# Layer 1's scores in a two-layer decoder trunk: the second half of the queries against all keys as three float32r products, on one core of a Trainium2 chip

## The chip, the cores and the metric

The kernel runs on one core of one Trainium2 chip. The metric is the device time of one execution in microseconds (us), as a median over runs. A core has five engines with a queue each, worked off in order: TensorE (PE: matrix products, into PSUM only), VectorE (DVE), ScalarE (ACT), GpSimd (POOL) and SyncE (SP, which here issues the loads). They run side by side and wait for each other by semaphores.

## The reference

A trunk of two layers over 256 tokens of 2048 features, all in float32. Each layer is a token mixer and a gated channel mixer. Layer 0's mixer is block attention, which for 256 tokens is plain causal attention; layer 1's is multi-head latent attention, and the change is there:

```python
cq = rms_norm(h @ wq_a, g_qa)
q = (cq @ wq_b).reshape(B, S, H, NOPE + RD)
q_nope = rms_norm(q[..., :NOPE], g_qn)
q_rope = rope(rms_norm(q[..., NOPE:], g_qr), pos, RD)
...
kv = (ckv @ wkv_b).reshape(B, S, H, NOPE + VD)
k_nope = rms_norm(kv[..., :NOPE], g_kn)
v = kv[..., NOPE:]
s = (jnp.einsum('bqhd,bkhd->bhqk', qn, k_nope)
     + jnp.einsum('bqhr,bkr->bhqk', qr, k_rope)).astype(F32) * scale
s = jnp.where(pos[None, :] <= q_pos[:, None], s, NEG_INF)
p = jax.nn.softmax(s, axis=-1).astype(v.dtype)
```

There are 16 heads with 128 plain and 64 rotary features each, and 128 value features.

## The kernel before

**Products and quanta.** Weights stream in from memory. A piece of 128 x 512 weights is split into a float32r part (`whi`, cast by ScalarE, L104) and the rest (`wlo`, subtracted by VectorE, L105); activations are split the same way. A product of full precision is then three float32r products: high by high, high by rest, rest by high. The work is a list of 1464 quanta, one piece each. Before quantum q, `ws.split` issues the casts of pieces up to four ahead; then come the quantum's matmuls (six of 512 columns in `tok_major`, L239, or twelve of 256 columns in `feat_major`, L265 to L267); then whatever was planned for this quantum: `first_in(q, ...)` (softmax transposes, values) ahead of `at(q, ...)`, and these in the order in which they were planned. Each engine's instructions stand in the order in which this loop issues them.

**Layer 1's attention** goes in four groups of four heads. A group has three or four kinds of four quanta each: keys, queries, values (the first group: queries, a half of the rotary queries, keys, values). Let K be the last quantum of a group's keys; its queries end at K+4, its values at K+8 and the next group's keys at K+12. For keys and for queries, `plan_heads` (L640) plans:

- `evac` (L365) at the kind's last quantum: ScalarE copies the two accumulators into a tile `qk`. There are two such tiles (L368, `bufs=2`), taken in turn by keys and queries.
- `squares` (L380) in the two quanta after it: four VectorE instructions for each half of the tokens, each with a readout, square and sum the heads one by one. (The first queries have a longer plan, `wide`.)
- `rstd` (L401) three quanta after it, on VectorE and GpSimd, and `scaled` (L411), on VectorE, five and six quanta after.
- `turned` (L455) and `turned_out` (L467) nine quanta after for heads 0 and 1, ten after for heads 2 and 3: four transposes into one PSUM bank `tp`, which one ScalarE instruction copies out with the gain, 128 x 512, into the tile `room`. There are two `tp` banks (`ps_tp`, `bufs=2`), and all transposes use them.

`room` takes the place of the tile `h`, which held the normed input; in it lie two sets of queries and keys, for even and odd groups, and three sets of values.

**A head** (`Head.plan`, L571): `scores` (L487) at quantum Q = K+15, +18, +21, +24 for the four heads of a group. For layer 1 the loop at L497 takes queries 0 to 127 by keys 0 to 127 and queries 128 to 255 by all 256 keys; each is one float32 product (L499), which PE runs in two passes, and two float32r products of the rotary part (L504). Then: masked maximum (`biased`, VectorE) at Q, `exps` (ScalarE) at Q+1, `normal` (VectorE) at Q+2, the transposes of the probabilities (`turn`, L533, into a `tp` bank; `turned`, L539, ScalarE copies them out) at Q+6, and `values` (L552) with `parted` at Q+9.

Layer 0 has its scores in three products already: `scores` has a branch for it (`self.parts`, L491 to L496), and `queries_out` (L603) and `keys_out` (L612) copy a bank out in three steps: ScalarE the high part, ScalarE a plain copy for the first half, VectorE the rest, `tp` minus the high part.

Of the kernel before, what the change touches and what calls it, by code (L numbers as in the profile page):

```python
# [48 lines left out]
BY_TOKEN, BY_FEATURE = (8, 8), (24, 56)  # L49

H_START = 8


class Stream:
# [61 lines left out]
def trunk(ctx: ExitStack, tc: tile.TileContext, a, out):  # L116
# [100 lines left out]
    def at(q, f, *args):  # L217
        side.setdefault(q, []).append((f, args))
# [51 lines left out]
    class Norm:  # L270
# [86 lines left out]
    class Heads:  # L357


        def __init__(self, state, n_heads, dh, gain, rot, tabs, scale, gain_column=None):  # L360
            self.gain_column = gain_column
# [26 lines left out]
        def squared(self):  # L388

            self.sq = []  # L390
            for t in range(NT):
                sq = att_pool.tile([P, 16 * 32], F32, name="ro2", bufs=2)
                nc.scalar.activation(sq, self.x[:, t].rearrange("p n d -> p (n d)"), AF.Square)
                self.sq.append(sq.rearrange("p (n d) -> p n d", n=self.n))

# [13 lines left out]
            nc.gpsimd.tensor_tensor(self.r, ms, mhalf[:, : NT * n], op=ALU.pow)  # L409

        def scaled(self, t):  # L411
            if self.gain_column is not None or self.gain is None:
                r = self.r[:, t * self.n : (t + 1) * self.n]
                nc.vector.tensor_tensor(
                    self.x[:, t], self.x[:, t], r[:, :, None].to_broadcast([P, self.n, self.dh]),
                    op=ALU.mult,
                )
                return
            g = gains[:, self.gain : self.gain + self.dh]
            for i in range(self.n):  # L420
                c = t * self.n + i
                nc.vector.scalar_tensor_tensor(
                    self.x[:, t, i], self.x[:, t, i], self.r[:, c : c + 1], g,
                    op0=ALU.mult, op1=ALU.mult,
                )
# [38 lines left out]
                    )  # L464
            pair["tp"] = tp

        def turned_out(self, dst, pair, i0):  # L467
            o = dst[:, i0 : i0 + 2, :].rearrange("p a s -> p (a s)")
            if self.gain_column is None:
                nc.scalar.copy(o, pair["tp"])  # L470
            else:
                c = self.gain_column
                nc.scalar.activation(o, pair["tp"], AF.Copy, scale=par[:, c : c + 1])

    def three(o, w_hi, w_lo, m_hi, m_lo, start, stop):

        mm(o, w_hi, m_hi, start=start, stop=False)  # L477
        mm(o, w_hi, m_lo, start=False, stop=False)  # L478
        mm(o, w_lo, m_hi, start=False, stop=stop)  # L479


    class Head:
# [4 lines left out]
        def scores(self):  # L487
            sc = ps_sc.tile([P, 512], F32, name="sc")
            qT, kT, i = self.qT(), self.kT(), self.i
            self.sc = sc  # L490
            if self.parts:  # L491

                (q0, q1), (k0, k) = qT, kT
                mm(sc[:, :P], q0[:, i], k0[:, i], start=True, stop=True)  # L494
                three(sc[:, P : 3 * P], q1[:, 0, i], q1[:, 1, i], k[:, 0, i], k[:, 1, i], True, True)
                return  # L496
            for q0, n, c in ((0, P, 0), (P, S, P)):  # L497
                o = sc[:, c : c + n]
                mm(o, qT[:, i, q0 : q0 + P], kT[:, i, :n], start=True, stop=self.rope is None)  # L499
                if self.rope is not None:  # L500

                    qr, kr = self.rope()
                    for part in range(2):
                        mm(o, qr[:, q0 : q0 + P], kr[:, part, :n], start=False, stop=part == 1)  # L504

        def biased(self):
            self.s = att_pool.tile([P, 3 * P], F32, name="s", bufs=3)
# [104 lines left out]
    def keys_out(dst, tp, i0):  # L612
# [4 lines left out]
        nc.scalar.copy(hi, src)  # L617
        nc.scalar.copy(k0[:, i0 : i0 + 2], src[:, :, :P])
        nc.vector.tensor_tensor(lo, src, hi.bitcast(F32), op=ALU.subtract)

    def evac_parts(state, key, scale):
        v0, v1 = env[key]
# [14 lines left out]
            else:  # L637
                nc.scalar.activation(dst, src, AF.Copy, scale=scale()[:, t : t + 1])

    def plan_heads(q, hs, key, step, out=None, late=0, wide=False):  # L640

        at(q, hs.evac)
        if wide:
            for t in range(NT):
                for i in (0, 2):
                    at(q + 1 + 2 * t + i // 2, hs.squares, t, range(i, i + 2))
                at(q + 8 + t, hs.scaled, t)
            at(q + 5, hs.rstd)
            for i0 in (0, 2):
                pair = {}  # L650
                q1 = q + 11 + i0 // 2
                at(q1, lambda p=pair, i0=i0: hs.turned(env[key], p, i0))
                at(q1, lambda p=pair, i0=i0: hs.turned_out(env[key], p, i0))
            return
        for t in range(NT):
            at(q + step * (1 + t), hs.squares, t)
        at(q + step * 3, hs.rstd)
        for t in range(NT):
            at(q + step * (5 + t) + late * (1 + t), hs.scaled, t)
            at(q + step * (5 + t) + late * (2 + t), hs.rotate, t)  # L660
        for i0 in (0, 2):
            pair = {}
            q1 = q + step * 9 + i0 // 2 + 2 * late
            at(q1, lambda hs=hs, p=pair, i0=i0, key=key: hs.turned(env[key], p, i0))
            if out is None:
                at(q1, lambda hs=hs, p=pair, i0=i0, key=key: hs.turned_out(env[key], p, i0))
            else:
                at(q1, lambda p=pair, i0=i0, key=key: out(env[key], p["tp"], i0))

    at(-1, n1.scaled, 0)  # L670
    at(9, load_constants)
    for g in range(4):
        for kind in "qkv":
# [13 lines left out]
            if kind == "v":  # L687
                at(q, evac_parts, state, ("v", g), lambda: n1.rstd)
                q_v = q
            else:  # L690
                hs = Heads(state, 4, P, G_Q if kind == "q" else G_K, 32, (tab, T_MC, T_MS), lambda: n1.rstd)
                plan_heads(q + (0 if g else 15 if kind == "q" else 9), hs, ("qT" if kind == "q" else "kT", g), 1,
                           queries_out if kind == "q" else keys_out, 1)
                q_k = q
        for i in range(4):
            hd = Head(
# [378 lines left out]
    at(q + 13, kr_turn)  # L1075

    def mla_tiles(g):
        i = 4 * (g % 2)
        env["qT", g] = env["room"][:, i : 4 + i]
        env["kT", g] = env["room"][:, 8 + i : 12 + i]  # L1080
        i = 4 * (g % 3)
        env["v", g] = env["room"][:, 16 + i : 20 + i].rearrange("p (t c) s -> p t (c s)", t=NT)

    for g in range(4):
        for kind in "kqv" if g else "qrkv":
            if kind == "r":
                rotary_queries(1, (6, 10, 12, 15, 16, 17, 18, 20, 21, 23, 24, 25, 26, 28, 40))
                continue
            state = {}
            for kt in range(4):  # L1090
                q = add(tok_major, state, lambda kind=kind: env["cqT" if kind == "q" else "ckvT"], kt, 3)
            if kind == ("k" if g else "q"):
                at(q, mla_tiles, g)
            if kind == "v":
                at(q, evac_values, state, ("v", g), None)
            else:
                q_q = q
                hs = Heads(state, 4, P, None, 0, None, (lambda: cq["scale"]) if kind == "q" else None,
                           C_GQN if kind == "q" else C_GKN)
# [143 lines left out]
```

## Time and profile before

| | us |
|---|---|
| median of 3 runs (2088.34 to 2089.35) | 2088.68 |
| the profiled execution | 2088.1 |
| its span, first to last instruction | 2086.1 |
| PE busy | 2081.1 |
| VectorE busy | 1407.1 |
| ScalarE busy | 1133.3 |

A line of a group reads: line of the kernel, engine, operation, output <- inputs, shapes, count | busy time in us, mean ns of one | idle time of the engine before it, and what ended that. In the chain of waits a line is: start, length, engine, tile, line of the kernel, count; lengths there run from end to end. In a timeline a length is the instruction's own, and instructions that follow each other overlap a little.

### The profile page before, as it was taken

How to read it: one execution, taken by the hardware profiler on the slowest of the kernel's cores; microseconds unless marked ns; L12 is line 12 of the kernel's file. 1: busy time of each engine (PE TensorE's matmuls, PEld its weight loads, DVE VectorE, ACT ScalarE, POOL GpSimd, SP SyncE). 2: the span in 40 equal slices, each digit the busy share in tenths (PEclk: the TensorE clock that was granted, in tenths of full speed). 3: DMA queues.
4: the chain of work that ended last, by engine and by line, in shares of the span. 5: the costliest groups of instructions: out<-in, count | busy, mean ns of one | idle time of the engine just before them, and what ended most of it. 6: DMA issues, size and time to landing. Idle time of an engine off the chain costs nothing.

```text
span 2086.1 us, 42075 instructions
## 1 busy us (share of the span) xinstructions
PE 2081.1 (100%) x16716; PEld 2012.4 (96%) x16716; DVE 1407.1 (67%) x3012; ACT 1133.3 (54%) x2199; POOL 46.1 (2%) x35
## 2 busy tenths in 40 slices
PE   9999999999999999999999999999999999999999
PEld 7888889999999999999999889999999999999999
DVE  6777776776666766655556886776676666755554
ACT  6555555555555555555455666655555555544443
POOL 0000000000000000000000110000000000000000
PEclk9999999999999999999999999999999999999999
DMA  7454445555555555555554533555555555555553
GB/s 274 162 182 176 168 162 202 183 194 190 202 186 200 191 194 199 191 197 189 197 202 154 200 122 122 183 201 185 200 193 191 200 187 200 190 202 208 195 207 132
DMA packets 59381, 391.81 MB, mean 188 GB/s; under 512 B 6960, under 2 KB 10032, under 8 KB 13232
## 3 DMA queue, kind: packets, MB, share of 16 engines
q1 hardware_dynamic: 59040, 388.87, 52.6%
q8 instruction: 130, 2.13, 0.4%
q14 instruction: 67, 0.55, 0.1%
q10 hardware_dynamic: 144, 0.26, 0.0%
HBM read 387.01 MB, written 2.10 MB: 187 GB/s over the span
## 4 chain that ended last, share of the span: by engine, by line
PE 99%; DMA 0%; SPq 0%; DVE 0%; ACT 0%; issue 0%
PE acc L265 26%; PE acc L267 26%; PE acc L266 26%; PE acc L239 17%; PE tp L462 1%; PE sc L499 1%; PE tp L536 1%; PE sc L561 0%; PE sc L504 0%; DMA xT<-in_xT 0%; PE sc L478 0%; PE sc L479 0%; PE sc L477 0%; PE sc L559 0%; PE sc L494 0%; PE sc L562 0%
## 5 line engine op out<-in xcount | busy, mean ns | idle before, releaser
L105 DVE TENSOR_TENSOR wlo<-raw,whi 128x512 fp32r<-128x512 f32 (+1 forms) x1464 | 999.5, 690 | 390.2 <-ACT whi L104 387.6
L104 ACT CAST whi<-raw 128x512 fp32r<-128x512 f32 (+1 forms) x1463 | 869.1, 619 | 456.3 <-PE acc L266 212.5
L265 PE MATMUL acc<-h,whi 128*128 128x256 f32 x2880 | 796.1, 276 | 0.0
L267 PE MATMUL acc<-h,wlo 128*128 128x256 f32 x2880 | 795.7, 276 | 0.0
L266 PE MATMUL acc<-h,whi 128*128 128x256 f32 x2880 | 795.6, 276 | 0.0
L266 PEld LDWEIGHTS acc<-h,whi 128*128 128x128 f32 x2880 | 540.8, 188 | 0.0
L267 PEld LDWEIGHTS acc<-h,wlo 128*128 128x128 f32 x2880 | 540.8, 188 | 0.0
L265 PEld LDWEIGHTS acc<-h,whi 128*128 128x128 f32 x2880 | 540.8, 188 | 0.0
L265 PE MATMUL acc<-a,whi 128*128 128x256 f32 x1408 | 389.0, 276 | 0.0
L266 PE MATMUL acc<-a,whi 128*128 128x256 f32 x1408 | 389.0, 276 | 0.0
L267 PE MATMUL acc<-a,wlo 128*128 128x256 f32 x1408 | 388.9, 276 | 0.0
L239 PE MATMUL acc<-whi,h 128*128 128x512 f32 (+1 forms) x896 | 272.6, 380 | 0.0
L267 PEld LDWEIGHTS acc<-a,wlo 128*128 128x128 f32 x1408 | 264.4, 188 | 0.0
L265 PEld LDWEIGHTS acc<-a,whi 128*128 128x128 f32 x1408 | 264.4, 188 | 0.0
L266 PEld LDWEIGHTS acc<-a,whi 128*128 128x128 f32 x1408 | 264.4, 188 | 0.0
L239 PEld LDWEIGHTS acc<-whi,h 128*128 128x128 f32 x896 | 164.8, 188 | 30.2 <-ACT whi L104 0.7
L239 PE MATMUL acc<-wlo,h 128*128 128x512 f32 (+1 forms) x448 | 168.8, 377 | 0.5 <-DVE wlo L105 0.5
L265 PE MATMUL acc<-oT,whi 128*128 128x256 f32 x512 | 142.7, 279 | 0.0
L267 PE MATMUL acc<-oT,wlo 128*128 128x256 f32 x512 | 141.7, 277 | 0.0
L266 PE MATMUL acc<-oT,whi 128*128 128x256 f32 x512 | 141.7, 277 | 0.0
L770 DVE TENSOR_TENSOR g<-acc,rstd_b 128x256 f32<-128x256 f32 x88 | 37.5, 426 | 125.4 <-PE acc L267 122.4
L777 ACT ACTIVATE c<-g,par 128x256 f32<-128x256 f32 x88 | 53.1, 603 | 108.3 <-DVE g L770 108.3
(163 smaller groups left out, 1599.6 us busy)
## 6 DMA issues: line engine op xcount, KB each, us to landing
raw<-in_ffn_gu SPq DMA_DIRECT2D x176, 1024.0 KB, 4.8
raw<-in_ffn_down SPq DMA_DIRECT2D x88, 1024.0 KB, 4.8
raw<-in_moba_wk SPq DMA_DIRECT2D x16, 1024.0 KB, 4.8
raw<-in_moba_wv SPq DMA_DIRECT2D x16, 1024.0 KB, 4.8
raw<-in_moba_wo SPq DMA_DIRECT2D x16, 1024.0 KB, 4.8
raw<-in_mla_wo SPq DMA_DIRECT2D x16, 1024.0 KB, 4.8
raw<-in_moba_wq SPq DMA_DIRECT2D x13, 1024.0 KB, 4.8
raw<-in_mla_wkv_a SPq DMA_DIRECT2D x8, 576.0 KB, 3.8
```

Source lines behind the costliest of these rows:

```text
L104: self.nc.scalar.copy(hi[:, :n], w)
L105: self.nc.vector.tensor_tensor(lo[:, :n], w, hi[:, :n].bitcast(F32), op=ALU.subtract)
L239: mm(state["acc"][t][:, :n], src[:, kt, c : c + P], (t_lo if part == 1 else t_hi)[:, :n], start=kt == 0 and part == 0, stop=kt == k_last a ...
L265: mm(o, w_hi, src[:, kt, :S], start=first and k == 0, stop=False, skip_group_check=True)
L266: mm(o, w_hi, src[:, kt, S:], start=False, stop=False, skip_group_check=True)
L267: mm(o, w_lo, src[:, kt, :S], start=False, stop=kt == k_last, skip_group_check=True)
L462: nc.tensor.transpose(tp[:, (i * NT + t) * P : (i * NT + t + 1) * P], flat[:, t, c : c + P], ident)
L499: mm(o, qT[:, i, q0 : q0 + P], kT[:, i, :n], start=True, stop=self.rope is None)
L536: nc.tensor.transpose(tp[:, c * P : (c + 1) * P], self.s[:, c * P : (c + 1) * P], ident)
L770: nc.vector.tensor_tensor(self.g[:, 2:], self.gate["acc"][:, :S], self.norm.rstd_b, op=ALU.mult)
L777: nc.scalar.activation(self.c, self.g[:, 2:], AF.Identity, bias=par[:, cb : cb + 1], scale=self.cw(2))
```

## The change

The plain scores of layer 1 take the form that layer 0 has: queries 0 to 127 by keys 0 to 127 stay one float32 product, queries 128 to 255 by all keys become three float32r products. So queries and keys are copied out in parts, with their gain (`queries_out`, `keys_out`). The squares are taken by ScalarE, a whole half of the tokens at once, and summed by one VectorE instruction. The tile `h` is split in two; its first half becomes `room` (plain queries, keys, values) and its second `rparts` (the parts), each with one place for queries and one for keys. A new plan, `plan_latent`, says when the steps run; the transposes of the second rotary queries run one quantum later.

```diff
+class Halves:
+    def __getitem__(self, at):
+        p, k, s = at
+        return self.tiles[k // 8][p, k % 8, s]
...
-                t = keep.tile([P, KD * 2 * S + 64], F32R, name="h")
-                self.h = t[:, H_START : H_START + KD * 2 * S].rearrange("p (k s) -> p k s", k=KD)
+                n = KD // 2 * 2 * S
+                tiles = [keep.tile([P, n + 64], F32R, name=f"h{i}") for i in range(2)]
+                self.h = Halves([
+                    t[:, H_START : H_START + n].rearrange("p (k s) -> p k s", k=KD // 2) for t in tiles
+                ])
...
-                sq = att_pool.tile([P, 16 * 32], F32, name="ro2", bufs=2)
+                sq = att_pool.tile([P, 16 * 32], F32, name="sq" if self.dh == P else "ro2", bufs=2)
                 nc.scalar.activation(sq, self.x[:, t].rearrange("p n d -> p (n d)"), AF.Square)
...
-            for q0, n, c in ((0, P, 0), (P, S, P)):
-                o = sc[:, c : c + n]
-                mm(o, qT[:, i, q0 : q0 + P], kT[:, i, :n], start=True, stop=self.rope is None)
-                if self.rope is not None:
-
-                    qr, kr = self.rope()
-                    for part in range(2):
-                        mm(o, qr[:, q0 : q0 + P], kr[:, part, :n], start=False, stop=part == 1)
+            (q0, q1), (k0, k) = qT, kT
+            first_, second = sc[:, :P], sc[:, P : 3 * P]
+            last = self.rope is None
+            flags = {} if last else {"skip_group_check": True}
+            mm(first_, q0[:, i], k0[:, i], start=True, stop=last, **flags)
+            three(second, q1[:, 0, i], q1[:, 1, i], k[:, 0, i], k[:, 1, i], last, last, **flags)
+            if last:
                 return
+            qr, kr = self.rope()
+            for o, t, n in ((first_, 0, P), (second, 1, S)):
+                for part in range(2):
+                    mm(
+                        o, qr[:, t * P : (t + 1) * P], kr[:, part, :n],
+                        start=False, stop=part == 1, **flags,
+                    )
...
+    def rest_of(lo, src, hi, gain):
+        if gain is None:
+            nc.vector.tensor_tensor(lo, src, hi.bitcast(F32), op=ALU.subtract)
+        else:
+            nc.vector.scalar_tensor_tensor(
+                lo, src, gain, hi.bitcast(F32), op0=ALU.mult, op1=ALU.subtract
+            )
...
-    def queries_out(dst, tp, i0):
+    def queries_out(dst, tp, i0, gain=None):
         q0, q1 = dst
         src = tp.rearrange("p (a t s) -> p a t s", a=2, t=NT)
         hi, lo = q1[:, 0, i0 : i0 + 2], q1[:, 1, i0 : i0 + 2]
-        nc.scalar.copy(hi, src[:, :, 1])
-        nc.scalar.copy(q0[:, i0 : i0 + 2], src[:, :, 0])
-        nc.vector.tensor_tensor(lo, src[:, :, 1], hi.bitcast(F32), op=ALU.subtract)
+        copied(hi, src[:, :, 1], gain)
+        copied(q0[:, i0 : i0 + 2], src[:, :, 0], gain)
+        rest_of(lo, src[:, :, 1], hi, gain)
...
     def open_room():
-        t = keep.tile([P, KD * 2 * S + 64], F32, name="room", tag="h")
-        env["room"] = t[:, : 32 * S].rearrange("p (k s) -> p k s", k=32)
+        n = KD // 2 * 2 * S
+        t = keep.tile([P, n + 64], F32, name="room", tag="h0")
+        env["room"] = t[:, :n].rearrange("p (k s) -> p k s", k=n // 512)
+        t = keep.tile([P, n + 64], F32R, name="rparts", tag="h1")
+        env["rparts"] = t[:, H_START : H_START + 3072].rearrange("p (k s) -> p k s", k=6)
...
+    def plan_latent(q, hs, key, out, sums, rest, turns):
+        at(q, hs.evac)
+        at(q + 1, hs.squared)
+        for t in range(NT):
+            at(q + sums + t, hs.sums, t)
+            at(q + rest + (2 if rest < 5 else 3) + t, hs.scaled, t)
+        at(q + rest, hs.rstd)
+        for i0, turn in zip((0, 2), turns):
+            pair = {}
+            at(q + turn, lambda p=pair, i0=i0: hs.turned(None, p, i0))
+            at(q + turn, lambda p=pair, i0=i0: out(env[key], p["tp"], i0))
...
-                rotary_queries(1, (6, 10, 12, 15, 16, 17, 18, 20, 21, 23, 24, 25, 26, 28, 40))
+                rotary_queries(1, (6, 10, 12, 15, 16, 17, 18, 20, 21, 23, 24, 25, 26, 29, 41))
...
-                plan_heads(q, hs, ("qT" if kind == "q" else "kT", g), 1, wide=(g, kind) == (0, "q"))
+                c, put, turns = (
+                    (C_GQN, queries_out, (9, 12)) if kind == "q" else (C_GKN, keys_out, (10, 14))
+                )
+                if g == 0:
+                    turns = (11, 12) if kind == "q" else (9, 10)
+                plan_latent(
+                    q, hs, ("qT" if kind == "q" else "kT", g), with_gain(put, c), 2,
+                    5 if (g, kind) == (0, "q") else 3, turns,
+                )
```

`keys_out` changes as `queries_out` does, with a high part and a rest of 128 x 512. The remaining lines drop arguments that nothing uses any more.

More of the change, by code (lines that the diff above doesn't have):

```diff
@@ L51, with __init__ @@
 H_START = 8
+class Halves:
+    def __init__(self, tiles):
+        self.tiles = tiles
+    def __getitem__(self, at):
+        p, k, s = at
+        return self.tiles[k // 8][p, k % 8, s]
 class Stream:
@@ L357, in trunk, with __init__ @@
     class Heads:
-        def __init__(self, state, n_heads, dh, gain, rot, tabs, scale, gain_column=None):
-            self.gain_column = gain_column
+        def __init__(self, state, n_heads, dh, gain, rot, tabs, scale):
             self.state, self.n, self.dh, self.gain = state, n_heads, dh, gain
@@ L411, in scaled @@
         def scaled(self, t):
-            if self.gain_column is not None or self.gain is None:
+            if self.gain is None:
                 r = self.r[:, t * self.n : (t + 1) * self.n]
@@ L465, in turned, with three @@
             pair["tp"] = tp
[L467 to L479, printed above, removed]
+    def three(o, w_hi, w_lo, m_hi, m_lo, start, stop, **flags):
+        mm(o, w_hi, m_hi, start=start, stop=False, **flags)
+        mm(o, w_hi, m_lo, start=False, stop=False, **flags)
+        mm(o, w_lo, m_hi, start=False, stop=stop, **flags)
     class Head:
@@ L601, in moba_tiles, with copied @@
         )
-    def queries_out(dst, tp, i0):
+    def copied(dst, src, gain):
+        if gain is None:
+            nc.scalar.copy(dst, src)
+        else:
+            nc.scalar.activation(dst, src, AF.Copy, scale=gain)
+    def rest_of(lo, src, hi, gain):
+        if gain is None:
+            nc.vector.tensor_tensor(lo, src, hi.bitcast(F32), op=ALU.subtract)
+        else:
+            nc.vector.scalar_tensor_tensor(
+                lo, src, gain, hi.bitcast(F32), op0=ALU.mult, op1=ALU.subtract
+            )
+    def queries_out(dst, tp, i0, gain=None):
         q0, q1 = dst
@@ L616, in keys_out @@
         hi, lo = k[:, 0, i0 : i0 + 2], k[:, 1, i0 : i0 + 2]
-        nc.scalar.copy(hi, src)
-        nc.scalar.copy(k0[:, i0 : i0 + 2], src[:, :, :P])
-        nc.vector.tensor_tensor(lo, src, hi.bitcast(F32), op=ALU.subtract)
+        copied(hi, src, gain)
+        copied(k0[:, i0 : i0 + 2], src[:, :, :P], gain)
+        rest_of(lo, src, hi, gain)
     def evac_parts(state, key, scale):
@@ L638, in evac_values, with plan_heads @@
                 nc.scalar.activation(dst, src, AF.Copy, scale=scale()[:, t : t + 1])
-    def plan_heads(q, hs, key, step, out=None, late=0, wide=False):
+    def plan_heads(q, hs, key, out):
         at(q, hs.evac)
[L643 to L654, printed above, removed]
         for t in range(NT):
-            at(q + step * (1 + t), hs.squares, t)
-        at(q + step * 3, hs.rstd)
+            at(q + 1 + t, hs.squares, t)
+        at(q + 3, hs.rstd)
         for t in range(NT):
-            at(q + step * (5 + t) + late * (1 + t), hs.scaled, t)
-            at(q + step * (5 + t) + late * (2 + t), hs.rotate, t)
+            at(q + 6 + 2 * t, hs.scaled, t)
+            at(q + 7 + 2 * t, hs.rotate, t)
         for i0 in (0, 2):
             pair = {}
[L663 to L668, printed above, removed]
+            q1 = q + 11 + i0 // 2
+            at(q1, lambda hs=hs, p=pair, i0=i0: hs.turned(None, p, i0))
+            at(q1, lambda p=pair, i0=i0, key=key: out(env[key], p["tp"], i0))
     at(-1, n1.scaled, 0)
@@ L691, in trunk @@
                 hs = Heads(state, 4, P, G_Q if kind == "q" else G_K, 32, (tab, T_MC, T_MS), lambda: n1.rstd)
-                plan_heads(q + (0 if g else 15 if kind == "q" else 9), hs, ("qT" if kind == "q" else "kT", g), 1,
-                           queries_out if kind == "q" else keys_out, 1)
+                plan_heads(q + (0 if g else 15 if kind == "q" else 9), hs, ("qT" if kind == "q" else "kT", g),
+                           queries_out if kind == "q" else keys_out)
                 q_k = q
@@ L1077, in mla_tiles, with with_gain @@
     def mla_tiles(g):
[L1078 to L1082, printed above, removed]
+        room, parts = env["room"], env["rparts"]
+        env["qT", g] = (
+            room[:, 0].rearrange("p (i s) -> p i s", i=4),
+            parts[:, 4:6].rearrange("p k (i s) -> p k i s", i=4),
+        )
+        env["kT", g] = (
+            room[:, 1].rearrange("p (i s) -> p i s", i=4),
+            parts[:, :4].rearrange("p (k a) (b s) -> p k (a b) s", k=2, b=2),
+        )
+        i = 2 * (1 + g % 3)
+        env["v", g] = room[:, i : i + 2]
+    def with_gain(out, c):
+        return lambda dst, tp, i0: out(dst, tp, i0, par[:, c : c + 1])
+    def plan_latent(q, hs, key, out, sums, rest, turns):
[9 more added lines that the diff above has]
+            at(q + turn, lambda p=pair, i0=i0: out(env[key], p["tp"], i0))
     for g in range(4):
```

11 lines of the change are left out of this document (4 added, 7 removed).

## The prediction

> **What bounds the kernel now.** I read the page first: how busy each engine is, and the chain that ended last.
>
> ```profile
> span 2086.1 us, 42075 instructions
> ...
> PE 2081.1 (100%) x16716; PEld 2012.4 (96%) x16716; DVE 1407.1 (67%) x3012; ACT 1133.3 (54%) x2199; POOL 46.1 (2%) x35
> ...
> PE 99%; DMA 0%; SPq 0%; DVE 0%; ACT 0%; issue 0%
> ```
>
> PE is the bound from end to end. A change gains only what it takes off PE's own instructions, and loses whatever makes PE wait. So I went to the stage that is changed and asked how much room the others have there: busy time in a window, and who waits for whom.
>
> ```profile
> 1174.00:1283.00 109.00, 108.99 (x648) 95.63 (x648) 90.48 (x340) 77.47 (x179) 18.97 (x9) 1.00 0.37 131
> ...
> ACT s L519 <- DVE sst L515: 18.7, 13, 4.1
> ...
> PEld tp L462 <- DVE qk L414: 0.2, 1, 0.2
> ```
>
> The first row has PE, weight loads, VectorE, ScalarE, GpSimd: of 109 us VectorE works 90.5 and ScalarE 77.5. PE waits for next to nothing (0.2 us once, from 1180 to 1300, where no row names a load either), but VectorE is 83% full, and ScalarE's idle time is mostly waiting (18.7 us for softmax sums alone). A shifted order can make PE wait here.
>
> **The change part by part. What PE gains.** The chain, at a head of layer 0 and at one of layer 1:
>
> ```profile
> 83.74 0.12 PE sc L477
> 83.85 0.12 PE sc L478
> 83.97 0.12 PE sc L479
> ...
> 1240.58 0.43 PE sc L561 x2
> 1241.01 0.22 PE sc L562 x2
> 1241.23 0.33 PE tp L536 x3
> 1241.56 0.22 PE sc L499 x2
> 1241.78 0.18 PE sc L504 x2
> 1241.96 0.48 PE sc L499 x2
> 1242.44 0.23 PE sc L504 x2
> ...
> 1244.49 1.38 PE acc L239 x6
> 1245.87 0.44 PE tp L462 x4
> ```
>
> The second L499 (256 columns, float32, two passes) becomes three products at 0.12, 0.36 us. It takes 0.48 in the chain, but the same form of product takes 0.43 at L561, where its neighbours are of its own kind, and L504 ahead of it (0.18 where its second pair has 0.23) looks too short by as much. So each of 16 heads gains between 0.07 and 0.12 us; I take 0.08, nearer to L561: 1.3 us in all, ends 1.1 and 1.9. Transposes keep their number.
>
> **What ScalarE and VectorE get.** From the groups by form, and PE's transpose, for later:
>
> ```profile
> L473 ACT ACTIVATE room<-tp,par 128x512 f32<-128x512 f32 x16 | 11.0, 686 | 5.1 <-PE tp L462 5.1
> L928 ACT ACTIVATE ckvT<-tp,par 128x256 fp32r<-128x256 f32 x4 | 1.9, 475 | 2.3 <-PE tp L923 2.3
> L393 ACT ACTIVATE ro<-qr 128x512 f32<-128x512 f32 x2 | 1.2, 638 | 0.0
> ...
> L383 DVE CUSTOM_DVE_ANT_0 junk<-qk 128x128 f32<-128x128 f32 x64 | 14.9, 286 | 0.0
> L929 DVE SCALAR_TENSOR_TENSOR ckvT<-tp,par,ckvT 128x256 fp32r<-128x256 f32 x4 | 1.9, 485 | 0.5 <-ACT ckvT L928 0.2
> L397 DVE TENSOR_REDUCE ss<-ro 128x8 f32<-128x512 f32 x3 | 2.0, 678 | 0.0
> ...
> L462 PE MATMUL tp<-ident,qk 128*128 128x128 f32 x128 | 19.2, 273 | 0.0
> ```
>
> And a stretch of ScalarE's timeline, with one row of VectorE's:
>
> ```profile
> 1236.01 0.37 ACT L568 CAST oT<-sc 128x256 fp32r<-128x256 f32 x1
> 1236.27 0.49 ACT L542 COPY pT<-tp 128x384 f32<-128x384 f32 x1
> ...
> 1238.20 0.40 ACT L519 ACTIVATE s<-s,sst 128x128 f32<-128x128 f32 x1 [0.34 <-DVE sst L515]
> ...
> 1239.09 0.67 ACT L473 ACTIVATE room<-tp,par 128x512 f32<-128x512 f32 x1
> 1239.66 1.13 ACT L104 CAST whi<-raw 128x512 fp32r<-128x512 f32 x2
> ...
> 1241.97 1.08 ACT L376 COPY qk<-acc 128x512 f32<-128x512 f32 x2
> 1242.92 0.64 ACT L104 CAST whi<-raw 128x512 fp32r<-128x512 f32 x1
> ...
> 1240.30 0.69 DVE L105 TENSOR_TENSOR wlo<-raw,whi 128x512 fp32r<-128x512 f32 x1 [0.34 <-ACT whi L104]
> ```
>
> Queued back to back, an instruction occupies ScalarE 0.10 us less than its length (0.67, but the next starts 0.57 later). VectorE starts 0.03 after the first cast (0.62 long) ends: I take 0.03 for each hand-over.
>
> ScalarE: 16 squares at 0.54 (L393) add 8.6; 16 copies at 0.58 go, -9.3; for queries 16 copies of 128 x 256 at 0.37 (L928) add 6.0; for keys eight of 512 at 0.59 and eight of 256 at 0.37 add 7.7: 13.0 us more, 77.5 to 90.5 of some 108. VectorE: 64 squares at 0.21 (row 1203.71 below to 1204.56, four in 0.85) go, -13.6; 16 sums at 0.68, eight rests of 256 at 0.49 and eight of 512 at 0.73 (between 0.49 and twice that) add at most 20.6: 7.0 more at most. Both still fit on average; what counts is the order.
>
> **The wait that the new plan makes.** In the groups after the first, keys are turned 10 and 14 quanta after K, their last quantum; until now it was 9 and 10. The next group's keys are evacuated at K+12, into the `qk` tile of these keys, since two tiles are used in turn by keys and queries. So ScalarE's evacuation at K+12 must wait for PE's transposes of heads 2 and 3 at K+14; the changed program's instruction order, read engine by engine, has that wait. The evacuation of this place is row 1241.97; K+14's transposes end at 1245.87 + 0.44. ScalarE stands for about 4.3 us, in the third and the fourth group's evacuations: twice.
>
> What is queued behind it: the next cast, the exponentials of K+13, and the copies of queries 0 and 1, turned at K+13 into a `tp` bank. In the old form that bank was free after one copy; now it is free only after ScalarE's high part, ScalarE's plain copy and VectorE's rest. PE needs it for a head's softmax transposes at K+15 (the other bank holds keys 2 and 3). From the end of K+14's transposes: 0.03 + two evacuations 0.95 (1241.97 to 1242.92) + cast 0.51 + exponentials 0.89 (1238.20 to 1239.09) + high part 0.37 + plain copy 0.48 + 0.03 + rest 0.49 + 0.03 = 3.78 us until PE may start, and its first transpose ends 0.27 later, at 4.05. Without the wait PE would do six products of K+15 (1.38) and the values (0.43 + 0.22), and the first transpose would end 0.11 on, at 2.14. PE stalls **1.91 us, twice: 3.8**. Ends: 1.4 with exponentials half done before the stop (VectorE delivers their sums early), 2.4 where another cast slips between.
>
> What is late next: queries 2 and 3, turned at K+16, need the bank that the softmax transposes filled, free when ScalarE has copied the probabilities. ScalarE, from 3.13 (its plain copy, overlap off): two squares 1.08, cast 0.51, keys' high part 0.59, plain copy 0.37, cast 0.51, L568 0.26, L542 0.49, hand-over 0.03: 6.97, first transpose done at 7.24. PE: 4.05 + two transposes 0.22 + scores 1.03 + six products 1.38 + 0.11 = 6.79. Another **0.45, twice: 0.9** (ends 0 and 1.4). Further lateness of the same kind I put at 0.3 (0 to 0.6).
>
> **Casts that come late.** In the first group nothing is reused too early, but the squares stand between casts. The tightest place there, in four timeline rows:
>
> ```profile
> 1206.37 0.40 ACT L519 ACTIVATE s<-s,sst 128x128 f32<-128x128 f32 x1 [4.13 <-DVE sst L515]
> ...
> 1203.71 0.28 DVE L383 CUSTOM_DVE_ANT_0 junk<-qk 128x128 f32<-128x128 f32 x1
> ...
> 1204.56 0.68 DVE L105 TENSOR_TENSOR wlo<-raw,whi 128x512 fp32r<-128x512 f32 x1
> ...
> 1205.67 0.39 PE L239 MATMUL acc<-wlo,ckvT 128*128 128x512 f32 x1
> ```
>
> `wlo` is ready at 1205.24, PE takes it at 1205.67: 0.43 spare. New ahead of it: two squares on ScalarE (1.08); on VectorE the keys' rest and two sums (about 2.0) in place of eight squares (1.70). 1.4 later, less the spare 0.43: I take 0.9 (0, if idle time takes the squares in, to 1.6).
>
> The rest costs nothing: splitting `h` moves addresses by 64 elements with the same loads and matmuls, SP's weight loads keep their order, and GpSimd's powers and the rotary steps their number; the rotary transposes only run a quantum later, with PE's full queue as their cover, and if a bank is late there they are part of the 0.3.
>
> **The sum.** Stalls 3.8 + 0.9 + 0.3 + 0.9 = 5.9, less 1.3: +4.6 us on the profiled execution, 2088.1 (span 2086.1, 2.0 around it) to 2092.7. The median of the runs is 0.6 above that execution, so I forecast 2093.3.
>
> **The rivals.** *Absorbed:* ScalarE's stop costs PE nothing, because casts are up to four pieces ahead. For it: row 1206.37, where ScalarE idles 4.13 us and PE does not wait. Against it: there no bank hung on ScalarE. It decides if the bank for K+15 is free within 2.0 us of K+14's transposes: then PE keeps its gain, 2088.7 - 1.3 = 2087.4, not slower.
>
> *ScalarE becomes the bound:* its idle time is 31.5 us; the two stops take 8.6, and if the 18.7 of waiting for sums stays, 4.2 are left for 13.0 of new work. 8.8 lost, less 1.3: 2096.2. For it: VectorE, which gives those sums, gets no emptier. Against it: waits shrink when the waiting engine comes later.
>
> *The clock drops in the stalls.* At the very start PE ran slower, and at the end it stood still:
>
> ```profile
> 1.19 4.41 PE L176 MATMUL sc<-zeros 128*128 128x512 bf16 x10 [1.19 <-DVE zeros L173]
> ...
> 2084.00:2086.00 2.00, 0.00 (x0) 0.00 (x0) 0.00 (x0) 0.00 (x0) 0.00 (x0) 1.00 0.19 66
> ```
>
> Ten products of 512 columns took 4.41, where ten at 0.23 (six in 1.38) take 2.3: 2.1 us for a cold start. After each long stall that would be 4.2 in all, 2097.4. Against it: the granted clock is 1.00 in every window, also with PE idle for 2 us at the end. The Trainium skill (TensorE: Matmul & The Clock Gate, Part 1: The HAM clock gate) states that the clock halves only after an idle window of about 3.4 us; by that rule stalls of 1.9 us leave it up and this rival falls, and the trace agrees as far as its 1.00 goes.
>
> *The products don't get cheaper* (gain 0, where the shorter form pays for its first product's weights): 2093.3 + 1.3 = 2094.6. Against it: 0.12 each at layer 0.
>
> **How the numbers follow.** Forecast 0.62, own range 2091.3 to 2095.3; absorbed 0.18; ScalarE the bound 0.14; clock 0.03; no cheaper products 0.03. The range of 8 in 10 is 2089.0 to 2097.0: part-absorbed stalls below, the second rival above. About 0.2% (4.2 us) is what a measurement can tell from no change: slower begins at 2092.9, inside the forecast's range. Slower: 0.38 of the forecast, and the three rivals above it, 0.20, 0.58. Same: the forecast's 0.24 and 0.16, 0.40. Faster 0.02.
>
> **What would show it.** PE waiting about 1.9 us twice, some 29 us apart, at transposes of `s`, released by VectorE's new rest; ScalarE idle over 4 us ahead of a `qk` copy, ended by PE's `tp`; three score products at 0.12. No PE waits in layer 1's attention, or waits on `whi` and `wlo` alone, would prove it wrong.

## The result, and the profile after

The changed kernel takes 2094.45 us in the median of 9 runs (2093.31 to 2095.01), the kernel before 2088.68 (9 runs, 2088.34 to 2090.05): a ratio of 1.0026 (95% interval 1.0017 to 1.0035), slower by 5.8 us. The profiled execution took 2094.45 as well, with a span of 2092.4, 6.3 more than before.

From the page after: the span, the busy time of each engine, and the shares of the chain that ended last.

```profile
span 2092.4 us, 42044 instructions
...
PE 2081.6 (99%) x16732; PEld 2011.6 (96%) x16732; DVE 1411.8 (67%) x2916; ACT 1144.9 (55%) x2231; POOL 46.0 (2%) x35
...
PE 98%; ACT 1%; DVE 1%; DMA 0%; SPq 0%; issue 0%
```

PE is still the bound. It is as busy as before (2081.6 against 2081.1), while the span grew by 6.3: PE lost its time by standing still, and the chain now runs over ScalarE and VectorE for 2% of the span.

To see where, take two places that both kernels pass once: the first transposes of `ckv` ahead of layer 1's attention, and the last head's values behind it. The chain of waits of before (start, length, engine, tile, line), with the first and last score row of one late head between them:

```profile
1168.49 0.22 PE tp L923 x2
...
1294.57 0.22 PE sc L499 x2
...
1295.45 0.24 PE sc L504 x2
...
1307.35 0.43 PE sc L561 x2
```

The same of after:

```profile
1169.51 0.22 PE tp L932 x2
...
1294.89 0.22 PE sc L502 x2
1295.11 0.12 PE sc L482
...
1295.35 0.12 PE sc L484
1295.47 0.46 PE sc L510 x4
...
1313.70 0.43 PE sc L570 x2
```

Between the two places lie 138.86 us before and 144.19 after: **+5.33, and all of the change is in there**. I call this time the *stretch* from here on. The 1.02 by which the first place itself is later arose in the first 24 us, while the first loads came in; that it is scatter between runs is shown by a run below. One head's scores take 1.04 us (1294.89 to 1295.93) where they took 1.12: 0.08 gained, and the second and third product start 0.12 apart.

Who waits for whom after, from 1170 to 1310 (us in total, times, longest):

```profile
ACT qk L389 <- PE tp L475: 5.4, 2, 3.0
PEld tp L545 <- DVE rparts L623: 4.2, 3, 2.0
PE tp L545 <- DVE rparts L623: 3.5, 2, 1.8
...
PEld acc L250 <- DVE wlo L116: 2.1, 5, 0.9
...
PEld tp L475 <- ACT pT L551: 0.6, 1, 0.6
...
PE acc L250 <- DVE wlo L116: 0.5, 1, 0.5
```

These are the rows that the prediction named: ScalarE's evacuation into `qk` waits for PE's transposes, twice; PE's softmax transposes wait for VectorE's new rest, twice 1.8 us; and PE waits once for a late `wlo`. PE's timeline at the three places (in brackets the idle time, which counts only from the modelled end of the row above it):

```profile
1206.08 0.61 PE L250 MATMUL acc<-whi,ckvT 128*128 128x512 f32 x2
1207.18 0.50 PE L250 MATMUL acc<-wlo,ckvT 128*128 128x512 f32 x1 [0.48 <-DVE wlo L116]
...
1222.00 0.38 PE L571 MATMUL sc<-pT,room 128*128 128x128 f32 x2
1224.15 0.55 PE L545 MATMUL tp<-ident,s 128*128 128x128 f32 x3 [1.76 <-DVE rparts L623]
...
1251.88 0.38 PE L571 MATMUL sc<-pT,room 128*128 128x128 f32 x2
1254.03 0.55 PE L545 MATMUL tp<-ident,s 128*128 128x128 f32 x3 [1.77 <-DVE rparts L623]
```

From start to start L571 takes 2.15 where it takes 0.22 undisturbed: two stalls of 1.93 us, 29.9 us apart. The late `wlo` costs 1.10 less two products of 0.23: 0.64. So much of the stretch adds up: 3.86 + 0.64 - 1.28 (16 heads at 0.08) = 3.22 of 5.33. The other 2.11 were not added up one by one; the small waits behind the stalls are among them, such as the weight loads' 0.6 for `pT`.

ScalarE's timeline at the first long stall, and two rows of VectorE's:

```profile
1220.38 1.08 ACT L389 COPY qk<-acc 128x512 f32<-128x512 f32 x2 [2.37 <-PE tp L475]
...
1221.43 0.17 DVE L524 TENSOR_SCALAR sst<-sst 128x2 f32<-128x2 f32 x1
...
1221.86 0.41 ACT L528 ACTIVATE s<-s,sst 128x128 f32<-128x128 f32 x1
...
1223.61 0.48 DVE L623 SCALAR_TENSOR_TENSOR rparts<-tp,par,rparts 128x256 fp32r<-128x256 f32 x1 [0.58 <-ACT room L616]
```

ScalarE stands for 2.4 us, then works off evacuation, cast, exponentials and copies, and VectorE's rest frees the bank at 1224.1, when PE goes on. But the row of 1221.43 says something that the prediction had not seen: VectorE's row maxima in `sst`, which the exponentials need (the prediction and the expectations call them sums), are ready only at 1221.60, 0.26 ahead of them. Without the stop the exponentials could have started hardly earlier. The same rows in the fourth group:

```profile
1249.72 0.17 DVE L524 TENSOR_SCALAR sst<-sst 128x2 f32<-128x2 f32 x1
...
1250.26 1.07 ACT L389 COPY qk<-acc 128x512 f32<-128x512 f32 x2 [3.02 <-PE tp L475]
...
1251.74 0.41 ACT L528 ACTIVATE s<-s,sst 128x128 f32<-128x128 f32 x1
```

There the maxima are ready 1.85 us ahead of the exponentials, and ScalarE alone is late. So the two equal stalls might have different causes, and that is what the first experiments ask.

### The profile page after: what moved, and what is told of

Its sections match the earlier page's. It is cut to its first block, busy times and chain, and to the rows that moved or that the text cites. A ratio compares the mean times of both kernels' runs of the same rounds, so it can differ in the third digit from the quotient of the medians.

```text
span 2092.4 us, 42044 instructions
## 1 busy us (share of the span) xinstructions
PE 2081.6 (99%) x16732; PEld 2011.6 (96%) x16732; DVE 1411.8 (67%) x2916; ACT 1144.9 (55%) x2231; POOL 46.0 (2%) x35
## 3 DMA queue, kind: packets, MB, share of 16 engines
q8 instruction: 131, 2.15, 0.4%
## 4 chain that ended last, share of the span: by engine, by line
PE 98%; ACT 1%; DVE 1%; DMA 0%; SPq 0%; issue 0%
PE acc L276 26%; PE acc L278 26%; PE acc L277 26%; PE acc L250 17%; PE tp L475 1%; PE tp L545 0%; PE sc L502 0%; PE sc L570 0%; PE sc L510 0%; DVE wlo L116 0%; PE sc L482 0%; PE sc L484 0%; PE sc L483 0%; DMA xT<-in_xT 0%; ACT whi L115 0%; PE sc L568 0%
## 5 line engine op out<-in xcount | busy, mean ns | idle before, releaser
L278 PE MATMUL acc<-h,wlo 128*128 128x256 f32 x2880 | 794.9, 276 | 0.0
L278 PEld LDWEIGHTS acc<-h,wlo 128*128 128x128 f32 x2880 | 540.6, 188 | 0.0
L278 PE MATMUL acc<-a,wlo 128*128 128x256 f32 x1408 | 388.6, 276 | 0.0
L278 PEld LDWEIGHTS acc<-a,wlo 128*128 128x128 f32 x1408 | 264.3, 188 | 0.0
L278 PE MATMUL acc<-oT,wlo 128*128 128x256 f32 x512 | 141.7, 277 | 0.0
```

Source lines behind the costliest of these rows:

```text
L278: mm(o, w_lo, src[:, kt, :S], start=False, stop=kt == k_last, skip_group_check=True)
```

## The experiments

Theory A is the prediction's: ScalarE's stop makes both long stalls. Theory B: the stop decides in the fourth group alone, and in the third VectorE's queue, with rotary work in it, is just as late. Theory C: the stop is harmless, and the bank is only held longer because three instructions empty it now. The table has all runs; the median of before is that of the runs on the same chip.

| kernel | median, us | before, us | ratio (95%) | stretch, us | against before |
|---|---|---|---|---|---|
| the change | 2094.45 | 2088.68 | 1.0026 (1.0017, 1.0035) | 144.19 | +5.33 |
| third place for `qk` | 2091.91 | 2089.03 | 1.0014 (1.0005, 1.0023) | 142.14 | +3.28 |
| four rotary steps left out | 2093.60 | 2089.03 | 1.0023 (1.0014, 1.0032) | 144.52 | +5.66 |
| both | 2090.53 | 2089.03 | 1.0007 (0.9998, 1.0016) | 140.64 | +1.78 |
| keys turned at K+12 | 2090.95 | 2089.03 | 1.0009 (1.0000, 1.0018) | 140.84 | +1.98 |
| before, with the new turns | 2091.96 | 2088.69 | 1.0015 (1.0006, 1.0024) | 142.24 | +3.38 |
| before, with `h` in halves | 2088.78 | 2088.69 | 0.9999 (0.9990, 1.0008) | 138.86 | 0.00 |
| squares a quantum apart | 2092.92 | 2088.69 | 1.0020 (1.0012, 1.0029) | 142.62 | +3.76 |
| combined | 2087.94 | 2088.69 | 0.9997 (0.9988, 1.0006) | 138.16 | -0.70 |
| combined, one float32 product | 2088.61 | 2088.46 | 1.0002 (0.9993, 1.0011) | 138.91 | +0.05 |
| squares on VectorE | 2097.05 | 2088.46 | 1.0042 (1.0030, 1.0055) | 147.02 | +8.16 |

The stretch comes from one profile each, by the two rows shown above, and it resolves tenths that the medians can't.

**A third place for `qk`.** It takes ScalarE's wait away and leaves the rest.

```diff
-  self.x = att_pool.tile([P, NT, n, dh], F32, name="qk", bufs=2)
+  self.x = att_pool.tile([P, NT, n, dh], F32, name="qk", bufs=2 if self.gain is not None else 3)
...
-  sq = att_pool.tile([P, 16 * 32], F32, name="sq" if self.dh == P else "ro2", bufs=2)
+  if self.dh == P:
+      sq = env["sq"][t]
...
+  env["sq"] = [t[:, H_START + 3072 + 512 * i :][:, :512] for i in range(NT)]
```

> The changed kernel with a third place for the evacuated keys and queries (`qk`), so that ScalarE's evacuation at K+12 no longer waits for the transposes at K+14; the squares lie in the rest of the `rparts` tile, rounded to float32r, to make room. Theory A (ScalarE's stop causes both long stalls of PE): both stalls of 1.93 us go, with the waits behind them (0.8 and 0.7 us): 2094.5 - 5.3 = 2089.2. Theory B (the stop decides only in the fourth group; in the third VectorE's queue is as late): there the exponentials cannot begin before VectorE's sums, which end at 1221.60 in the changed kernel's trace, 0.26 ahead of the exponentials that started at 1221.86. So the third group's stall stays at 1.6 us or more; in the fourth the sums end at 1249.89 and the exponentials start at 1251.74, so 1.85 of its 1.93 go, with the 0.7 behind it: 2094.5 - 2.6 - 0.3 = 2091.6. Theory C (the bank is held longer because of its three copies, the stop is harmless): no change, 2094.5, both stalls at 1.9.

2091.91, where theory B said 2091.6 and theory A 2089.2 (the kernel before runs 0.35 higher on this chip than in the first comparison). Its waits from 1190 to 1290 have no row any more in which ScalarE's `qk` waits for PE's `tp`, and of the two waits of PE for the rest one:

```profile
PE tp L548 <- DVE rparts L626: 1.5, 1, 1.5
```

One long stall is left, that of the third group. ScalarE's and VectorE's timeline there:

```profile
1217.60 1.09 ACT L389 COPY qk<-acc 128x512 f32<-128x512 f32 x2
...
1221.14 0.17 DVE L527 TENSOR_SCALAR sst<-sst 128x2 f32<-128x2 f32 x1
...
1221.34 0.40 ACT L531 ACTIVATE s<-s,sst 128x128 f32<-128x128 f32 x1 [2.13 <-DVE sst L527]
```

The evacuation runs without a stop, and ScalarE then stands 2.13 us for VectorE's maxima instead. In the fourth group the stall is gone: the stop was its cause.

**Four rotary steps left out, and both.** The second edit leaves out four of VectorE's rotary instructions (the second 128 tokens of heads 8 to 15 stay unrotated), first on the changed kernel, then on the one with the third place.

```diff
   def rotate(t, stage):
+      if u == t == 1:
+          return
```

> The changed kernel without four of VectorE's rotary instructions (the second 128 tokens of heads 8 to 15 are left unrotated), which leaves VectorE 2.2 us less to do in the stretch of the third group's stall; ScalarE's stop is as before. Theory A and theory B both expect the third group's stall to stay near 1.9 us, because the stop alone is enough for it: 2094.5, at most 0.5 less. If VectorE's queue alone makes the third group's stall and the stop is harmless there, the stall falls to 1 us or less: about 2093.2. The fourth group, which has no rotary work, keeps its 1.9 by every theory.

> The third place for `qk` together with the four rotary instructions left out (the second 128 tokens of heads 8 to 15 are left unrotated). Theory A: the same as the third place alone, both long stalls gone, 2089.2. Theory B (either lateness is enough in the third group): only with both away does the third group's stall fall, to 1 us or less, below that of both runs that take away one alone; about 2090.4, 1.2 less than the third place alone. Theory C: both stalls at 1.9.

With the rotary steps away and the stop in place, the third group's stall is as long as ever. PE's timeline of that run:

```profile
1222.89 0.55 PE L545 MATMUL tp<-ident,s 128*128 128x128 f32 x3 [1.76 <-DVE rparts L623]
```

With both away it is 0.62:

```profile
1223.98 0.55 PE L548 MATMUL tp<-ident,s 128*128 128x128 f32 x3 [0.62 <-DVE rparts L626]
```

1.76 with either one left to it, or nearly (1.51), and 0.62 with neither: each of the two latenesses is enough by itself, as theory B has it. The run with both away took 2090.53, where theory B said 2090.4. The run with the rotary steps left out was 0.85 below the change, and 1.2 by the distances to before, more than the 0.5 allowed for: with VectorE emptier small waits behind the third group's stall go too (the 0.6 for `pT` is not among its waits), but they were not added up. The stretch of its profile, +5.66, does not show this gain, because it holds a drop of PE's clock that cost 1.6 (last section); without it +4.06 would be left, 1.3 less than in the change.

**Keys turned at K+12.** One number: heads 2 and 3 are turned as soon as the last score has read their place.

```diff
-  else (C_GKN, keys_out, (10, 14))
+  else (C_GKN, keys_out, (10, 12))
```

> The changed kernel with keys of heads 2 and 3 turned at K+12 instead of K+14, right after the last score that reads their one place; one number is changed. ScalarE's evacuation at K+12 then waits only for transposes of the same quantum, 0.5 us or less. Theory A: both long stalls and what follows them go, 2089.2. Theory B: the fourth group's go, the third group's stays at 1.6 or more in one place or another: about 2091.6. In both a new short wait is possible: at K+12 softmax and keys fill both `tp` banks, so the queries' transposes at K+13 wait for the copy of the probabilities, under 0.8 us. Theory C: 2094.5.

2090.95, between the two theories' numbers and nearer to B. No stall is left in the fourth group, and in the third PE waits in two other places, both times for VectorE. PE's timeline:

```profile
1216.53 0.66 PE L475 MATMUL tp<-ident,qk 128*128 128x128 f32 x4 [0.42 <-DVE rparts L623]
...
1230.36 0.55 PE L545 MATMUL tp<-ident,s 128*128 128x128 f32 x3 [0.58 <-DVE rparts L623]
```

The second of them is the long stall of old, now 0.6 and one head later; the expectation of 1.6 or more for theory B was too high.

**The kernel before with the new turns alone.** Two places, whole products and one copy per turned pair stay; only the stop comes in.

```diff
   q1 = q + step * 9 + i0 // 2 + 2 * late
+  if late == 0 and (key[0] == "kT" and key[1] or key[0] == "qT"):
+      q1 = q + ((14 if i0 else 10) if key[0] == "kT" else (12 if i0 else 9))
```

> The kernel before with nothing but the new turns in the second, third and fourth groups (queries 9 and 12, keys 10 and 14 quanta after their last one); two places for queries and keys, whole products, squares on VectorE and one copy per turned pair stay. It has ScalarE's stop at K+12, but a `tp` bank that is free after one copy. Stop alone (theory A and B for the fourth group): from the end of K+14's transposes 0.03 + evacuations 0.95 + cast 0.51 + exponentials 0.89 + one copy 0.57 + 0.03 until PE may turn the softmax: 2.98, against 2.14 - 0.27 = 1.87 without a wait, a stall of 1.1 us in place of 1.93, in both groups: 2088.7 + 2.2 = 2090.9, up to 2091.5 with follow-ons. So 0.8 of each long stall is the two further instructions that hold the bank. Theory C (only the longer hold): no stall, 2088.7. If the stop does nothing in the third group (VectorE sets the time there), a stall in the fourth alone: 2089.8.

The waits of that run from 1190 to 1290:

```profile
ACT qk L376 <- PE tp L462: 7.8, 2, 4.3
...
PE tp L536 <- ACT room L473: 2.2, 2, 1.1
```

Two stalls of 1.1 idle, as worked out (1.27 from start to start), released by ScalarE's copy. The time, 2091.96, is 0.5 above the top of the expectation: of the stretch's 3.38 the two stalls are 2.54, and PE also waits once for a late `wlo` here (0.3 us), which the expectation did not have. So the stop alone does harm, also in the third group, and theory C falls. Set against the changed kernel's 1.76, 0.66 of each stall is left for the two further instructions on the bank, where 0.8 was expected; no run has these two alone, so that share is argued and not shown. The stop is the 4.3 us of the prediction here, once, and 3.5 the other time; in the changed kernel ScalarE has more to do ahead of it, arrives later and stands 2.4 and 3.0.

**The kernel before with `h` in halves.**

```diff
-  t = keep.tile([P, KD * 2 * S + 64], F32R, name="h")
+  n = KD // 2 * 2 * S
+  tiles = [keep.tile([P, n + 64], F32R, name=f"h{i}") for i in range(2)]
...
```

> The kernel before with `h` in two tiles and nothing else of the change (queries, keys and values of layer 1 keep all their places in the two halves). The prediction gave this part nothing: 2088.7, the same as before within 0.2%. The rival: the 1.0 us that the changed kernel's profile lost within its first 24 us belongs to the split: 2089.7, and a later first `h` in the trace.

2088.78 against 2088.69. The two places in its chain of waits:

```profile
1169.19 0.22 PE tp L937 x2
...
1308.05 0.43 PE sc L575 x2
```

138.86 us, before's stretch to the hundredth, although the first place is 0.70 later than in before's profile. Over all the runs it lies between 0.25 earlier and 2.0 later: that part is scatter of the start, and the split costs nothing.

**Squares a quantum apart.** One square and not two stands ahead of a cast.

```diff
...
-  at(q + 1, hs.squared)
+  hs.sq = []
   for t in range(NT):
+      at(q + 1 + t, hs.squared, t)
       at(q + sums + t, hs.sums, t)
```

> The changed kernel with ScalarE's two squares of a tile in two quanta instead of one, so that one square (0.54 us) and not two stand ahead of a cast. If the squares make the first group's late cast, its stall of 0.65 us falls to 0.1; the stalls of the third and fourth group stay: 2094.5 - 0.5 = 2094.0. If it is VectorE's own new work (the keys' rest and the sums), the 0.65 stays: 2094.5.

Three times the gain expected: the stretch is 1.57 shorter, the median's distance to before 1.5. Its waits of PE from 1190 to 1290:

```profile
PE tp L546 <- DVE rparts L624: 3.5, 2, 1.8
PEld acc L250 <- DVE wlo L116: 0.7, 3, 0.4
```

The wait of PE itself for `wlo` is gone from the first group, as expected; the long stalls are unchanged. The other 0.9 comes from behind them, where the pair of squares (1223.46, 1.15 us, in the changed kernel) also stood ahead of the casts and copies that PE needed next.

**Combined.** Keys at K+12, squares apart, and the second rotary set moved so that VectorE has less in its queue in the third group.

```diff
...
-  rotary_queries(1, (6, 10, 12, 15, 16, 17, 18, 20, 21, 23, 24, 25, 26, 29, 41))
+  rotary_queries(1, (6, 9, 13, 16, 18, 19, 22, 24, 25, 30, 32, 33, 34, 38, 41))
...
```

> The change with three repairs: keys of heads 2 and 3 turned at K+12, the two squares of a tile in two quanta, and the second set of rotary queries worked on later (its eight VectorE rotary steps at 19, 22, 24, 25, 30, 32, 33 and 34 quanta and not 17 to 26, its first turn at 38), so that VectorE has less to do in the third group. If the causes found so far (stop, VectorE's rotary work, two squares in one place) are all there is, PE keeps its 1.3 us and loses at most 0.7 in short waits: 0.6 to 1.3 below before, 2087.5 to 2088.3. If ScalarE or VectorE is the bound in this stage, the waits only move: 2090 or more.

2087.94, 0.75 below before, inside the forecast; the interval takes in 1, so this is no measured gain on before, but 6.5 below the change by the distances to before. The longest waits of PE's side from 1190 to 1290 are now those of its weight loads:

```profile
PEld tp L476 <- DVE rparts L624: 0.5, 1, 0.5
...
PEld sc L511 <- DVE qrT L1026: 0.2, 1, 0.2
```

ScalarE is as busy as in the changed kernel (1145.0 us against 1144.9), so it was never the bound. The rotary steps' new places were not tried alone.

**Combined, one float32 product.** One product of the high parts in place of the three; the low parts are left out of these scores.

```diff
-  three(second, q1[:, 0, i], q1[:, 1, i], k[:, 0, i], k[:, 1, i], last, last, **flags)
+  if last:
+      three(second, q1[:, 0, i], q1[:, 1, i], k[:, 0, i], k[:, 1, i], last, last, **flags)
+  else:
+      mm(second, q1[:, 0, i].bitcast(F32), k[:, 0, i].bitcast(F32), start=False, stop=False, **flags)
```

> The combined kernel with one float32 product of the high parts in place of the three float32r products (the low parts are left out of the scores), everything else the same. If three products gain 0.08 us a head, as the changed kernel's scores show (17.90 us for all score products before, 16.62 after, 16 heads), this is 1.3 slower than the combined kernel: 2087.9 + 1.3 = 2089.2. If the products are no cheaper, the two are equal, 2087.9.

A head's scores in its chain of waits:

```profile
1294.66 0.22 PE sc L503 x2
1294.88 0.43 PE sc L507 x2
1295.31 0.46 PE sc L514 x4
```

1.11 us, against 1.04 with three products: the product takes 0.43, not 0.36, and a gain of 0.07 to 0.08 a head is real. The stretch grew by 0.75 only, not by 1.3. Of the combined kernel's short waits, the 0.5 of the weight loads for VectorE's rest is gone; where the other part went was not traced. By the distances to before, the medians say 0.9, with intervals wider than that.

**Squares on VectorE.**

```diff
-  at(q + 1, hs.squared)
   for t in range(NT):
-      at(q + sums + t, hs.sums, t)
+      at(q + 1 + t, hs.squares, t)
```

> The changed kernel with the squares of queries and keys on VectorE again (64 at 0.21 us for 16 sums at 0.60: VectorE gets 3.8 us more, ScalarE 8.6 less). If ScalarE's squares make the late cast of the first group, its 0.65 us go and the rest stays: 2093.8. If VectorE is the fuller engine, the casts come later still, in the first group 1 us or more and after the long stalls too: 2095 to 2097. The two long stalls keep 1.9 each by both, and each is one more look at whether PE's clock drops after them, as it did once of the seven seen so far, for 3.4 us.

2097.05, just past the top of the 2095 to 2097 expected if VectorE is the fuller engine, and 2.8 more over before than the change. Its waits from 1190 to 1290:

```profile
PE tp L545 <- DVE rparts L623: 3.5, 2, 1.8
...
PE acc L250 <- DVE wlo L116: 2.7, 3, 1.2
```

The long stalls stay, and PE's waits for late casts grow from 0.5 to 2.7, with another 0.9 at L278, where the changed kernel has none. VectorE is the fuller engine; moving the squares to ScalarE was the right direction, at a wrong place.

## Why the prediction was right, point by point

The forecast was 2093.3 and slower as the likeliest sign, the time 2094.45. On the profiled execution it was +4.6 for the change's part, and the stretch shows +5.33.

- **PE's gain.** 0.08 a head, 1.3 in all: measured 0.08 by the rows of one head, and by putting the whole product back.
- **The main wait.** Two stalls of 1.91 forecast, two of 1.93 measured, at the place, in the groups and with the releaser named. The step that failed is inside it: "ScalarE stands for about 4.3 us, in the third and the fourth group's evacuations: twice", as the one cause of both. ScalarE stood 2.4 and 3.0, and in the third group VectorE's maxima were nearly as late as the stop made ScalarE, so removing the stop there gained 0.25 and not 1.9. The prediction weighed only that they might come early. The sum hid this, because two latenesses side by side cost no more than one; that VectorE stayed 0.26 short of the stop, so that 1.91 fits the third group too, is luck.
- **What follows.** 0.9 and 0.3 were set down, and 2.11 are left when the other terms are taken off: the term that was mis-sized most, and the reason why the forecast is low. It worked out one wait for a bank behind each stall, with the pair of squares in it, and put all further ones at 0.3; setting the squares apart alone gave back 0.9.
- **Casts that come late.** 0.9 forecast, 0.64 measured, and gone with the squares apart.
- **The rest costs nothing.** Shown for the split of `h`; the other parts were not tried alone.
- **The rivals.** Absorption fell: the bank was not free in time. ScalarE did not become the bound: with the same work well placed the kernel is level with before. "No cheaper products" fell. The clock, given 0.03 (its time is 2097.5 by its own terms, not 2097.4), did not drop in the changed kernel's profile, but it can drop: see the last section.

## What to carry to other kernels

An edit that saves a place in memory can move the last use of a buffer past its next fill; list for every tile of a rotation the last reader and the next writer, in the order of issue, before counting instructions. Where a stall has a plausible cause, look at the other inputs of the first instruction behind it: if one of them is ready only 0.26 us earlier, removing the cause gains 0.26 us. And a stall that runs over three engines ends in small waits behind it: beside the two long stalls and one late cast 2.1 of the 5.3 us were left here, and setting the pairs of squares apart gave back 0.9 of them.

## What the runs showed of the hardware

PE's clock fell after a stall of less than 2 us. In the run with the rotary steps left out the fourth group's stall had 1.78 us of idle time, like the others, and then the windows of its profile (width, busy time of PE, weight loads, VectorE, ScalarE, GpSimd, granted clock, DMA share, GB/s) read:

```profile
1253.00:1254.00 1.00, 1.00 (x9) 0.92 (x8) 0.82 (x3) 1.00 (x4) 0.00 (x0) 0.87 1.04 442
1254.00:1255.50 1.50, 1.50 (x5) 1.18 (x4) 1.50 (x4) 1.50 (x5) 0.00 (x0) 0.50 0.55 229
1255.50:1257.00 1.50, 1.50 (x7) 1.25 (x6) 1.50 (x6) 0.25 (x1) 0.00 (x0) 0.50 0.00 0
1257.00:1258.00 1.00, 1.00 (x6) 0.82 (x5) 0.96 (x4) 0.93 (x3) 0.00 (x0) 0.93 0.00 0
```

Half the clock for 3.4 us (0.26 + 3.0 + 0.14), from about 1.6 us after PE had gone on. Its chain shows the price: six products that take 1.38 and four transposes that take 0.44 elsewhere.

```profile
1253.73 2.45 PE acc L250 x6
1256.18 0.85 PE tp L475 x4
1257.03 1.51 PE acc L250 x6
```

1.07 + 0.41 + 0.13 = 1.6 us. The Trainium skill (TensorE: Matmul & The Clock Gate, Part 1: The HAM clock gate) has the clock halve after an idle window of about 3.4 us, by which the prediction ruled this out. The length of the drop agrees with that window; the condition does not fit, since only 1.78 us of idle time came before this drop. Of the nine long stalls profiled (1.5 to 1.8 idle) it was the only one followed by a drop, with others of the same length in the same place, so what decides was not found.

The mean granted clock of the other runs is on record too. One such drop takes 3.4 us at half the clock out of some 2091, so a run that has one shows 0.999 in place of 1.000, though 0.999 alone does not prove one. Three of the nine runs of the change show it (2094.20, 2094.80 and 2095.01; the other six have a median of 2094.26). So do two of the ten with the rotary steps left out, one of eleven each with the squares apart and with the new turns alone, and 2 of 81 of the kernel before, whose profile has no such stall. Leaving these runs out moves no median of the table by more than about 0.2 us. That a long stall is what brings such a drop is not shown.
